# Attention's instructions on three engines tied to a written order, scores in two parts around the transposes, normalization a step later

## Chip, core and metric

One Trainium2 chip; the program runs on one of its cores. The metric is the device time of one execution in microseconds (us). A core has TensorE (PE in the profile, its weight loads PEld), VectorE (DVE), ScalarE (ACT), GpSimd (POOL) and SyncE (SP). Each engine takes its own instructions in the order in which they stand in its stream; an instruction that waits holds up all that stand behind it on that engine.

## What is computed

One layer of a streaming encoder on 1024 tokens of width 1024: a projection to queries, keys, values and an SSM input; differential attention over 4 heads of two score maps each; an S5 state-space mixer with a gated linear unit (GLU); an output projection with layer norm; a mixture of 32 experts with a second layer norm. The change touches attention, the end of the GLU and nothing else:

```python
# per block of 128 queries, head h, the two maps c = 0, 1 (chunk-block-causal mask)
sc = einsum('bqhcd,bkhcd->bhcqk', qi, k) * scale
p = softmax(where(mask, sc, -inf))
attn = p[:, :, 0] - lam * p[:, :, 1]
o = einsum('bhqk,bkhe->bqhe', attn, v)
o = o * rsqrt(mean(o**2) + RMS_EPS) * subln_g * (1 - lam_init)
# GLU behind the S5 mixer
z = gelu(y); z = z * sigmoid(z @ w_glu + b_glu)
```

## The kernel before

Attention is cut into 32 units (h, i): head h and the block i of 128 queries, which sees n = 128(i+1) keys. `units` lists heads 0 and 1 first, alternating a wide block of head 0 with a narrow one of head 1, (0,7), (1,0), (0,6), (1,1), ..., and then heads 2 and 3 together from block 7 down to block 0. In what follows unit u is the u-th of this list, counted from 0, and step u is one turn of the loop over them, which computes the scores of unit u+2 (`LEAD` is 2) and weighs the values of unit u.

- `scores` (L781 to L811): TensorE multiplies queries and keys into a tile `s` (L792 and L793, each product in two parts for precision). VectorE sets the masked corner (L801 or L809) and takes the negative maximum into `nm` (L802 or L810). ScalarE takes the exponential into `p` and its sum into `L` (L795). With n up to 512 both maps share one `s` tile; with more each map has one, and the three engines are gone through once for each map. The `s` tiles come from `bank2`, which has two buffers.
- `weigh` (L814 to L830): VectorE takes the reciprocal of `L`, a small factor `rho` and then p0 + rho p1 (all through the helper `stt`, L163). TensorE transposes the result (`at`, L826); ScalarE copies the first four blocks of it from PSUM and VectorE the others (L827); TensorE multiplies by the values into `po` (L830). Four blocks of a head share one `po`.
- `normalize` (L832 to L855): after a group of four blocks ScalarE copies `po` and squares it, VectorE sums and scales in small instructions on 128x4 numbers (`ss`), GpSimd takes the power -1/2 and multiplies. `finish` transposes (`ot`, L852) and ScalarE writes `aoT` (L853).
- `FILLS` puts other work behind given steps: `ask` (queries of heads 2 and 3, with casts on ScalarE, subtractions on GpSimd and DMAs), `glu_prepare` (loads w_glu into `wg_raw`, casts on ScalarE, subtractions on GpSimd), eight `glu` parts (12 products each on TensorE, a tanh on ScalarE, a scaling on GpSimd, and a multiplication of `zT` on VectorE) behind steps 16 to 19 and 21 to 24, and `wo_part` (four quarters of w_out through `wo_raw`).

The 128x2048 tiles of all these are slots of a first-in, first-out list (`Slots`), so a load waits until the tile that had its slot before has been read. What sets the order within attention is the compiler's scheduler, which merges all of this by its own estimates of time. Only behind the routing, in the experts, does the kernel write its order out: `keep_order` there makes each instruction follow the one traced before it on its engine. After attention come the output projection (`mix`, L1082) with the routing and then the experts.

Of the kernel before, what the change touches and what calls it, by code (L numbers as in the profile page):

```python
# [19 lines left out]
P = 128  # L20
# [93 lines left out]
def tile_kernel(ctx: ExitStack, tc: tile.TileContext, I: dict, out: bass.AP, dbg=None):  # L114
# [624 lines left out]
    def glu(ct, half):  # L739
# [12 lines left out]
        mul(z_, z_, sg)  # L752
# [10 lines left out]
    ts(gcol, gcol, 1.0 - LAM_INIT, ALU.mult)  # L763
    aoT = {}

    def sm(name, n, bufs=4):
        return cp.tile([P, n], F32, tag=name, name=name, bufs=bufs)

# [14 lines left out]
    def scores(h, i, qd, L, j):  # L783
# [13 lines left out]
        if n <= 512:  # L797
            s2 = bank2(f"s{h}_{i}").rearrange("p (c n) -> p c n", c=2)
            for c in range(2):
                products(s2[:, c, :], c)  # L800
            V.memset(s2[0:64, :, n - 64:n], -1e30)  # L801
            V.tensor_reduce(out=nm, in_=s2[:, :, 0:n], axis=AX.X, op=ALU.max, negate=True)  # L802
            for c in range(2):
                weights(s2[:, c, :], c)
        else:
            for c in range(2):
                s_ = bank2(f"s{h}_{i}_{c}")
                products(s_, c)
                V.memset(s_[0:64, n - 64:n], -1e30)  # L809
                V.tensor_reduce(out=nm[:, c:c + 1], in_=s_[:, 0:n], axis=AX.X, op=ALU.max, negate=True)  # L810
                weights(s_, c)  # L811
        return p_

    def weigh(h, i, p_, L, RL, j, po):  # L814
# [5 lines left out]
        stt(p_[:, 0, 0:n], p_[:, 1, 0:n], rho, p_[:, 0, 0:n], ALU.mult, ALU.add)  # L820
        aT = half.get("aT", [8, P], bufs=2)
# [6 lines left out]
        sl.put(p_)  # L828
        for k in range(i + 1):
            PE.matmul(po[:, j * P:(j + 1) * P], aT[:, k, :], vv[k // 4][:, k % 4, h * P:(h + 1) * P],  # L830
                      start=(k == 0), stop=(k == i))

    def normalize(h, g, po, RL):
# [5 lines left out]
        ss = sm("ss", 4, 2)  # L839
        V.tensor_reduce(out=ss, in_=sq[:, 0, :].rearrange("p (j e) -> p j e", j=4), axis=AX.X, op=ALU.add)  # L840
        r0 = RL[:, :, 0]
        mul(ss, ss, r0)
        mul(ss, ss, r0)
        ts(ss, ss, 1.0 / P, ALU.mult, EPS, ALU.add)
        G.tensor_tensor(out=ss, in0=ss, in1=mhalf, op=ALU.pow)
        mul(ss, ss, r0)
        mul(o4, o4, ss.unsqueeze(2).broadcast_to([P, 4, P]), G)
# [7 lines left out]
        return finish  # L855
# [16 lines left out]
    def start(u):  # L872
# [6 lines left out]
        live[u] = scores(h, i, qd[h], grp[h, i // 4][0], i % 4)  # L879
        starts[h] = starts.get(h, 0) + 1  # L880
        if starts[h] == NT:
            sl.put(*qd.pop(h), kk.pop(h))

# [19 lines left out]
    late = {}  # L903
    for u in range(LEAD):
        start(u)
    for u, (h, i) in enumerate(units):
        if u + LEAD < len(units):
            start(u + LEAD)
        L_, RL_, po_ = grp[h, i // 4]
        weigh(h, i, live.pop(u), L_, RL_, i % 4, po_)  # L910
# [3 lines left out]
        if ends[h, i // 4] == 4:  # L914
            late[u + LATE] = normalize(h, i // 4, po_, RL_)
        if u in fills:
            for f_, *a_ in fills[u]:
                {"ask": ask, "pre": glu_prepare, "glu": glu, "wo": wo_part}[f_](*a_)
    for f_ in late.values():
        f_()  # L920
    sl.put(*vv.values())
# [418 lines left out]
    def keep_order():  # L1340

        traced, prev = nc.cur_bb.bb.instructions, {}
        at = next(k for k, i in enumerate(traced) if i is pins[0])
        for i in traced[at:]:
            if i.engine not in ORDERED:
                continue
            if i.engine in prev:
                tc.add_manual_dep(i, prev[i.engine].name,
                                  mybir.DependencyInfo(mybir.DependencyClass.NoSync, mybir.DependencyReason.DATA),
                                  reason="keep_order")  # L1350
            prev[i.engine] = i
# [273 lines left out]
```

## Time and profile before

| what | us |
|---|---|
| median of 3 runs | 1177.47 (1177.21 to 1180.05) |
| profiled execution | 1178.13 |
| its span in the trace | 1176.4 |
| scores of unit 2 to scores of unit 31 (attention's body) | 282.93 to 416.24 |
| first product of the output projection | 417.94 |

Over the whole span TensorE is busy 92%, VectorE 82%, ScalarE 60%, GpSimd 30%. The shares are means over stages of different kind: the projection and the SSM come first, then attention from 273 to about 440 us, the projection out and the routing to about 560 us, and then the experts, in which TensorE is busy nearly throughout. Times within the trace are counted from the start of the span. A row of the timeline gives start, duration, engine, source line, operation, output and inputs, and in brackets how long the engine sat idle before it and what ended that.

### The profile page before, as it was taken

How to read it: one execution, taken by the hardware profiler on the slowest of the kernel's cores; microseconds unless marked ns; L12 is line 12 of the kernel's file. 1: busy time of each engine (PE TensorE's matmuls, PEld its weight loads, DVE VectorE, ACT ScalarE, POOL GpSimd, SP SyncE). 2: the span in 40 equal slices, each digit the busy share in tenths (PEclk: the TensorE clock that was granted, in tenths of full speed). 3: DMA queues.
4: the chain of work that ended last, by engine and by line, in shares of the span. 5: the costliest groups of instructions: out<-in, count | busy, mean ns of one | idle time of the engine just before them, and what ended most of it. 6: DMA issues, size and time to landing. Idle time of an engine off the chain costs nothing.

```text
span 1176.4 us, 15227 instructions
## 1 busy us (share of the span) xinstructions
PE 1083.7 (92%) x5345; PEld 903.9 (77%) x5345; DVE 970.0 (82%) x1434; ACT 708.5 (60%) x956; POOL 358.0 (30%) x296
## 2 busy tenths in 40 slices
PE   6979998897869989995999999999999999999994
PEld 5867887676758878885888888888888888888862
DVE  4898567556878785456899999999999999999976
ACT  3312332426756653212788888888888888888852
POOL 1077464312453454243121221221221211211133
PEclk9989999898999999996999999999999999999997
DMA  8537321201120346446599999999999999999593
GB/s 209 138 97 259 113 59 29 59 19 41 40 64 4 130 160 217 168 171 242 195 343 386 374 380 389 382 393 392 367 393 381 362 384 379 387 392 386 191 261 149
DMA packets 90686, 278.90 MB, mean 237 GB/s; under 512 B 29468, under 2 KB 49964, under 8 KB 66160
## 3 DMA queue, kind: packets, MB, share of 16 engines
q1 hardware_dynamic: 78080, 252.78, 57.6%
q0 software_dynamic: 11520, 24.83, 7.8%
q8 instruction: 43, 0.70, 0.2%
q10 hardware_dynamic: 1008, 0.30, 0.1%
q14 instruction: 35, 0.29, 0.1%
HBM read 254.12 MB, written 34.60 MB: 245 GB/s over the span
## 4 chain that ended last, share of the span: by engine, by line
PE 69%; DVE 12%; DMA 7%; ACT 4%; SPq 3%; issue 3%; POOL 1%; ACTq 0%; DVEq 0%; POOLq 0%
PE g L1251 15%; PE y L1242 15%; PE u L1251 14%; PE mix L1082 7%; PE proj L243 4%; DMA misc<-in_w_in_dram 3%; PE xT L1212 3%; DMA moe_dram<-zero 2%; PE glu L745 2%; PE po L830 2%; DVE ssm L157 1%; SPq L581 1%; PE hT L1224 1%; PE s L792 1%; PE pl L1104 1%
## 5 line engine op out<-in xcount | busy, mean ns | idle before, releaser
L1151 POOL DMA_INDIRECT moe_dram<-yo,idx x30 | 52.1, 1738 | 425.9 <-DVE yo L163 425.9
L243 PE MATMUL proj<-xh,wa 128*128 128x512 f32 x256 | 77.9, 412 | 4.4 <-ACT ssm L678 4.2
L243 PE MATMUL proj<-xh,wb 128*128 128x512 f32 x256 | 74.5, 404 | 1.6 <-ACT ssm L678 1.6
L1082 PE MATMUL mix<-woh,mx 128*128 128x512 f32 x256 | 73.8, 399 | 1.6 <-DVE mx L154 1.6
L1146 POOL DMA_INDIRECT gx<-h_dram,idx x32 | 60.4, 1889 | 22.5 <-DVE WT L160 13.1
L795 ACT ACTIVATE p<-s,nm 128x1024 f32<-128x1024 f32 (+7 forms) x64 | 47.2, 743 | 24.3 <-DVE nm L810 14.9
L243 PEld LDWEIGHTS proj<-xh,wa 128*128 128x128 f32 x256 | 50.2, 199 | 14.9 <-ACT ssm L678 4.5
L243 PEld LDWEIGHTS proj<-xh,wb 128*128 128x128 f32 x256 | 48.6, 194 | 11.5 <-ACT ssm L678 1.8
L1082 PEld LDWEIGHTS mix<-woh,mx 128*128 128x128 f32 x256 | 47.4, 189 | 11.2 <-DVE mx L154 2.1
L792 PE MATMUL s<-kk,qh 128*128 128x512 f32 (+3 forms) x96 | 37.6, 396 | 18.1 <-ACT p L795 15.0
L1258 ACT ACTIVATE yo<-y,WT 128x1024 f32<-128x1024 f32 (+1 forms) x33 | 36.0, 1091 | 24.4 <-PE y L1242 24.4
L1212 PEld LDWEIGHTS xT<-ident,gx 128*128 128x128 f32 x256 | 36.2, 208 | 9.7 <-DMA gx<-h_dram,idx 5.7
L243 PE MATMUL proj<-xl,wa 128*128 128x512 f32 x128 | 43.6, 412 | 0.0
L1212 PE MATMUL xT<-ident,gx 128*128 128x128 f32 x256 | 36.9, 287 | 6.9 <-DMA gx<-h_dram,idx 5.4
L163 DVE SCALAR_TENSOR_TENSOR yo<-gx,first,yo 128x1024 f32<-128x1024 f32 (+1 forms) x33 | 41.3, 1252 | 1.6
L154 DVE TENSOR_TENSOR xe<-xT,xe 128x1024 fp32r<-128x1024 f32 (+1 forms) x33 | 39.1, 1184 | 4.1 <-ACT xe L173 4.1
L830 PE MATMUL po<-vv,half 128*128 128x128 f32 x288 | 41.0, 285 | 1.4 <-ACT half L827 1.3
L1082 PE MATMUL mix<-wol,mx 128*128 128x512 f32 x128 | 42.1, 397 | 0.0
L243 PE MATMUL proj<-xl,wb 128*128 128x512 f32 x128 | 41.0, 397 | 0.0
L173 ACT CAST xe<-xT 128x1024 fp32r<-128x1024 f32 (+1 forms) x33 | 32.3, 978 | 13.4 <-PE xT L1212 13.4
L830 PEld LDWEIGHTS po<-vv,half 128*128 128x128 f32 x288 | 37.4, 198 | 3.5 <-ACT half L827 2.4
L792 PEld LDWEIGHTS s<-kk,qh 128*128 128x128 f32 x96 | 19.3, 201 | 24.7 <-ACT p L795 22.6
(864 smaller groups left out, 3560.1 us busy)
## 6 DMA issues: line engine op xcount, KB each, us to landing
misc<-in_w_in_dram SPq DMA_DIRECT2D x16, 512.0 KB, 3.9
moe_dram<-zero SPq DMA_DIRECT2D x8, 1024.0 KB, 8.5
xr<-in_x_dram SPq DMA_DIRECT2D x8, 512.0 KB, 8.8
wo_raw<-in_w_out_dram SPq DMA_DIRECT2D x4, 1024.0 KB, 5.1
xa<-in_x_dram SPq DMA_DIRECT2D x8, 512.0 KB, 4.4
h_dram<-xa SPq DMA_DIRECT2D x8, 512.0 KB, 3.6
mo<-moe_dram SPq DMA_DIRECT2D x8, 512.0 KB, 8.6
mo<-moe_dram POOLq DMA_DIRECT2D x8, 512.0 KB, 12.7
```

The lines of the kernel that those rows point to most:

```text
L154: eng.tensor_tensor(out=out_, in0=a, in1=b, op=ALU.subtract)
L163: return V.scalar_tensor_tensor(out=out_, in0=a, scalar=s, in1=b, op0=op0, op1=op1)
L243: PE.matmul(o[:, hs], wt[kt // 4][:, w_, kt % 4, :], x_[:, hs], start=(kt == 0 and n == 0), stop=(kt == KT - 1 and n == 2))
L792: PE.matmul(s_[:, c0:c0 + w], qd[0][:, c, tk], kk[h][:, c, c0:c0 + w], start=True, stop=False)
L795: S.activation(p_[:, c, 0:n], s_[:, 0:n], AF.Exp, bias=nm[:, c:c + 1], accum_out=L[:, j, c:c + 1])
L830: PE.matmul(po[:, j * P:(j + 1) * P], aT[:, k, :], vv[k // 4][:, k % 4, h * P:(h + 1) * P], start=(k == 0), stop=(k == i))
L1082: PE.matmul(o[-(hs.start > 0)][:, hs], mx[:, m_, kt, :], (woh, wol)[w_][kt // 2][:, kt % 2, hs], start=(kt == 0 and n == 0), stop=(kt == K ...
L1146: return G.indirect_dma_start(out=dst, out_offset=None, in_=h_dram[:, :], in_offset=bass.IndirectOffsetOnAxis(ap=ix, axis=0), bounds_check ...
L1151: G.indirect_dma_start(out=moe_dram[:, :], out_offset=bass.IndirectOffsetOnAxis(ap=ix, axis=0), in_=src, in_offset=None, bounds_check=2 * ...
L1212: PE.transpose(b_[:, kt * P:(kt + 1) * P], rows(g_, kt), ident)
L1242: PE.matmul(y[h_], hid[e][:, x_, kt, :], w_[:, k, HALVES[h_]], start=(kt == 0 and n == 0), stop=(kt == 3 and n == 2))
L1251: PE.matmul(o, xT[e][:, x_, kt, :], w_[:, k, :], start=(kt == 0 and n == 0), stop=(kt == KT - 1 and n == 2))
```

## The change

- A new function `tie` holds the loop that `keep_order` had, and is called for attention too: every instruction of TensorE, ScalarE and VectorE that is traced from the first unit's scores to the last `finish` must follow the one traced before it on its engine. Left out of it are the instructions of `ask`, `glu_prepare` and `wo_part`; those of `glu` are in it. GpSimd and SyncE aren't tied.
- `scores`, `start` and `weigh` become generators, and the loop interleaves them by hand: (1) VectorE's part of `weigh` for unit u; (2) scores of unit u+2, of the first map where n is over 512, of both maps otherwise, with maximum and exponential; (3) transposes of unit u and their copies; (4) `normalize` of a group that ended a step earlier; (5) the second map's scores; (6) the sums and the scaling of that normalization; (7) the products with the values of unit u; then `finish`, then fills.
- `normalize` is given `L` in place of its reciprocal: it adds 128 eps L0^2 to the sum of squares (two small instructions for it and one addition), in place of three multiplications and a two-operation scaling, with sqrt(128) moved into `gcol`.
- The GLU's last multiplication goes from VectorE to GpSimd.

```diff
@@ glu
-        mul(z_, z_, sg)
+        mul(z_, z_, sg, G)
@@
-    ts(gcol, gcol, 1.0 - LAM_INIT, ALU.mult)
+    ts(gcol, gcol, (1.0 - LAM_INIT) * math.sqrt(P), ALU.mult)
+    def tie(traced, engines):
+        prev = {}
+        for i in traced:
+            if i.engine not in engines:
+                continue
+            if i.engine in prev:
+                tc.add_manual_dep(i, prev[i.engine].name,
+                                  mybir.DependencyInfo(mybir.DependencyClass.NoSync, mybir.DependencyReason.DATA),
+                                  reason="keep_order")
+            prev[i.engine] = i
@@ scores
             for c in range(2):
                 weights(s2[:, c, :], c)
-        else:
-            for c in range(2):
...
+            yield p_
+        for c in range(2 if n > 512 else 0):
+            s_ = bank2(f"s{h}_{i}_{c}")
+            products(s_, c)
...
+            weights(s_, c)
+            yield p_
@@ weigh
         stt(p_[:, 0, 0:n], p_[:, 1, 0:n], rho, p_[:, 0, 0:n], ALU.mult, ALU.add)
+        yield
...
         sl.put(p_)
+        yield
         for k in range(i + 1):
             PE.matmul(po[:, j * P:(j + 1) * P], aT[:, k, :], vv[k // 4][:, k % 4, h * P:(h + 1) * P],
@@ normalize
-        ss = sm("ss", 4, 2)
-        V.tensor_reduce(out=ss, in_=sq[:, 0, :].rearrange("p (j e) -> p j e", j=4), axis=AX.X, op=ALU.add)
-        r0 = RL[:, :, 0]
-        mul(ss, ss, r0)
-        mul(ss, ss, r0)
-        ts(ss, ss, 1.0 / P, ALU.mult, EPS, ALU.add)
-        G.tensor_tensor(out=ss, in0=ss, in1=mhalf, op=ALU.pow)
-        mul(ss, ss, r0)
-        mul(o4, o4, ss.unsqueeze(2).broadcast_to([P, 4, P]), G)
+        ss, l2 = sm("ss", 4, 2), sm("l2", 4, 2)
+        mul(l2, L[:, :, 0], L[:, :, 0])
+        ts(l2, l2, EPS * P, ALU.mult)
+        def scale():
+            V.tensor_reduce(out=ss, in_=sq[:, 0, :].rearrange("p (j e) -> p j e", j=4), axis=AX.X, op=ALU.add)
+            add(ss, ss, l2)
+            G.tensor_tensor(out=ss, in0=ss, in1=mhalf, op=ALU.pow)
+            mul(o4, o4, ss.unsqueeze(2).broadcast_to([P, 4, P]), G)
@@ the loop
-        if u + LEAD < len(units):
-            start(u + LEAD)
-        weigh(h, i, live.pop(u), L_, RL_, i % 4, po_)
+        old = weigh(h, i, live.pop(u), L_, RL_, i % 4, po_)
+        new = start(u + LEAD) if u + LEAD < len(units) else iter(())
+        next(old)
+        next(new, None)
+        next(old)
+        scales = [normalize(*done.pop(x)) for x in list(done)]
+        next(new, None)
+        for sc, fin in scales:
+            sc()
+            late[u + LATE - 1] = fin
+        next(old)
...
+                if f_ != "glu":
+                    apart.update(range(at, len(nc.cur_bb.bb.instructions)))
...
+    tie([i for k, i in enumerate(nc.cur_bb.bb.instructions) if k >= first_pin and k not in apart],
+        (mybir.EngineType.PE, mybir.EngineType.Activation, mybir.EngineType.DVE))
```

Three places show what this does to the streams. The first is TensorE at step 20, unit (2,5), while the scores of unit 23, (3,4), are next. In the names s_4_0 and s_4_1 are the first and second map's scores of a block 4, at_5 the transposes of a block 5, po_7_2596 (po_7_2600 after the change) the product with the values of head 2, and kk_2065 the keys of head 3. Before:

```order
L826 MATMUL at_5_0_2964<-ident,p_5_2824 128x128 x4
L792 MATMUL s_4_0_2988<-kk_2065,qh_2544 128x512
L793 MATMUL s_4_0_2988<-kk_2065,ql_2545 128x512
L792 MATMUL s_4_0_2988<-kk_2065,qh_2544 128x128
L793 MATMUL s_4_0_2988<-kk_2065,ql_2545 128x128
L826 MATMUL at_5_4_2970<-ident,p_5_2824 128x128 x2
L792 MATMUL s_4_1_2996<-kk_2065,qh_2544 128x512
L793 MATMUL s_4_1_2996<-kk_2065,ql_2545 128x512
L792 MATMUL s_4_1_2996<-kk_2065,qh_2544 128x128
L793 MATMUL s_4_1_2996<-kk_2065,ql_2545 128x128
L826 MATMUL at_5_0_3008<-ident,p_5_2886 128x128 x4
L830 MATMUL po_7_2596<-vv_1403,half_2070 128x128 x4
```

The product with the values of unit 20 stands behind both parts of unit 23's scores and behind transposes of unit 21. After:

```order
L839 MATMUL at_5_0_2956<-ident,p_5_2828 128x128 x4
L839 MATMUL at_5_4_2962<-ident,p_5_2828 128x128 x2
L804 MATMUL s_4_1_2966<-kk_2006,qh_2324 128x512
L805 MATMUL s_4_1_2966<-kk_2006,ql_2325 128x512
L804 MATMUL s_4_1_2966<-kk_2006,qh_2324 128x128
L805 MATMUL s_4_1_2966<-kk_2006,ql_2325 128x128
L844 MATMUL po_7_2600<-vv_1403,half_2070 128x128 x4
L844 MATMUL po_7_2600<-vv_1404,half_2070 128x128 x2
L804 MATMUL s_4_0_2992<-kk_2065,qh_2544 128x512
L805 MATMUL s_4_0_2992<-kk_2065,ql_2545 128x512
L804 MATMUL s_4_0_2992<-kk_2065,qh_2544 128x128
L805 MATMUL s_4_0_2992<-kk_2065,ql_2545 128x128
```

It now stands directly behind the second part of unit 22's scores, and unit 23's scores stand behind it. The second place is ScalarE at the same steps. Before:

```order
L795 ACTIVATE p_4_2942,L<-s_4_0_2944,nm 128x640
L749 ACTIVATE wg_raw<-glu_0_2926,bg 128x512
L795 ACTIVATE p_4_2942,L<-s_4_1_2952,nm 128x640
L827 COPY half_2070<-at_5_0_2964 128x512
L173 CAST woh_3100<-wo_raw_3098 128x1024
L795 ACTIVATE p_4_2986,L<-s_4_0_2988,nm 128x640
L827 COPY half_2070<-at_5_0_3008 128x512
```

Both exponentials of unit 22 come ahead of the copy of unit 20's transposes. After:

```order
L749 ACTIVATE wg_raw<-glu_0_2926,bg 128x512
L807 ACTIVATE p_4_2946,L<-s_4_0_2948,nm 128x640
L840 COPY half_2070<-at_5_0_2956 128x512
L807 ACTIVATE p_4_2946,L<-s_4_1_2966,nm 128x640
L173 CAST woh_3090<-wo_raw_3088 128x1024 x2
L807 ACTIVATE p_4_2990,L<-s_4_0_2992,nm 128x640
```

The copy has moved between the two exponentials of unit 22. The third place is ScalarE around steps 12 and 13, where the casts of w_glu (`wgh`) and of the SSM's output (`zh`) stand, and s_7_0 is the first part of unit 15's scores. Before:

```order
L795 ACTIVATE p_0_2523,L<-s_0_2525,nm 128x128 x2
L173 CAST zh_2696<-zT_763 128x1024
L173 CAST zh_2696<-zT_1282 128x1024
L827 COPY half_2070<-at_6_0_2576 128x512
L173 CAST wgh<-wg_raw 128x1024 x2
L795 ACTIVATE p_7_2554,L<-s_7_0_2556,nm 128x1024
```

After:

```order
L807 ACTIVATE p_0_2527,L<-s_0_2529,nm 128x128 x2
L840 COPY half_2070<-at_1_0_2538 128x256
L173 CAST wgh<-wg_raw 128x1024 x2
L173 CAST zh_2686<-zT_763 128x1024
L173 CAST zh_2686<-zT_1282 128x1024
L807 ACTIVATE p_7_2558,L<-s_7_0_2560,nm 128x1024
```

All four casts now stand ahead of unit 15's first exponential, and the copy of at_6 has gone behind it.

## Rows read from the trace of the kernel before

**Rows 1.** Stretches: length, busy us of PE, PEld, DVE, ACT, POOL, clock, DMA share, GB/s.
```profile
282.93:416.24 133.31, 111.51 (x691) 96.60 (x691) 110.51 (x228) 85.82 (x182) 53.99 (x41) 0.97 0.21 64
352.00:416.24 64.24, 59.28 (x367) 51.74 (x367) 52.35 (x108) 40.74 (x84) 25.48 (x20) 1.00 0.25 82
```
**Rows 2.** Timeline of TensorE: first products of units 2, 18 and 31.
```profile
282.93 0.79 PE L792 MATMUL s<-kk,qh 128*128 128x512 f32 x1 [2.13 <-ACT p L795]
...
352.00 0.50 PE L792 MATMUL s<-kk,qh 128*128 128x512 f32 x1
...
416.24 0.33 PE L792 MATMUL s<-kk,qh 128*128 128x128 f32 x1 [3.06 <-DVE p L163]
```
**Rows 3.** Chain that ended last: start, us; a value product, a GLU part, a score.
```profile
355.36 2.75 PE glu L745 x12
358.10 0.23 PE s L792
...
358.90 0.89 PE po L830 x8
```
**Rows 4.** Timeline of all engines: hand-overs from engine to engine.
```profile
302.75 0.40 PE L793 MATMUL s<-kk,ql 128*128 128x512 f32 x1
...
303.51 1.23 DVE L802 TENSOR_REDUCE nm<-s 128x2 f32<-128x1024 f32 x1
...
304.83 0.69 ACT L795 ACTIVATE p<-s,nm 128x512 f32<-128x512 f32 x1
...
309.50 0.59 ACT L827 COPY half<-at 128x512 f32<-128x512 f32 x1
...
310.14 1.16 PE L830 MATMUL po<-vv,half 128*128 128x128 f32 x8
```
**Rows 5.** Groups by line, 270 to 445 us: count, busy us, mean ns, idle before.
```profile
L795 ACT ACTIVATE p<-s,nm 128x1024 f32<-128x1024 f32 (+7 forms) x64 | 47.2, 743 | 24.3 <-DVE nm L810 14.9 <-DVE nm L802 7.0 <-DVE RL L817 2.1
...
L810 DVE TENSOR_REDUCE nm<-s 128x1 f32<-128x1024 f32 (+3 forms) x32 | 32.5, 1017 | 0.4
...
L827 ACT COPY half<-at 128x512 f32<-128x512 f32 (+3 forms) x32 | 16.2, 506 | 21.8 <-PE at L826 21.8
...
L802 DVE TENSOR_REDUCE nm<-s 128x2 f32<-128x256 f32 (+3 forms) x16 | 13.1, 818 | 0.3
...
L173 ACT CAST woh<-wo_raw 128x1024 fp32r<-128x1024 f32 x8 | 8.1, 1053 | 3.3 <-DMA wo_raw<-in_w_out_dram 2.7 <-DVE zT L157 0.6
...
L157 DVE TENSOR_TENSOR ss<-ss,RL 128x4 f32<-128x4 f32 x23 | 7.4, 325 | 2.3 <-POOL ss L845 2.1
L157 POOL TENSOR_TENSOR half<-half,ss 128x512 f32<-128x512 f32 x7 | 7.3, 1043 | 7.1 <-DVE RL L817 4.0 <-DVE ss L157 3.1
L157 DVE TENSOR_TENSOR zT<-zT,wg_raw 128x512 f32<-128x512 f32 x8 | 7.0, 872 | 0.6 <-POOL wg_raw L169 0.5
```
**Rows 6.** Groups by line and shape: widest and narrowest exponential with n over 512.
```profile
L795 ACT ACTIVATE p<-s,nm 128x1024 f32<-128x1024 f32 x8 | 8.9, 1113 | 4.4 <-DVE nm L810 4.4
...
L795 ACT ACTIVATE p<-s,nm 128x640 f32<-128x640 f32 x8 | 6.4, 796 | 5.2 <-DVE nm L810 4.2 <-DVE RL L817 0.9
```
**Rows 7.** SyncE's queue, waits: total us, times, longest.
```profile
SPq L729 <- PE s L793: 100.6, 1, 100.6
```
**Rows 8.** Chain that ended last, at the load of w_glu.
```profile
332.19 5.62 DMA wg_raw<-in_w_glu_dram
```
**Rows 9.** Timeline of all engines, VectorE beside GpSimd's subtraction.
```profile
321.31 2.62 DVE L163 SCALAR_TENSOR_TENSOR rho<-L,nlam,RL 128x1 f32<-128x1 f32 x1
321.53 4.79 POOL L154 TENSOR_TENSOR ql<-qr,qh 64x1024 fp32r<-64x1024 f32 x2
...
323.97 3.17 DVE L163 SCALAR_TENSOR_TENSOR p<-p,rho 128x768 f32<-128x768 f32 x1
```
**Rows 10.** Stretch of 10 us with the gap before unit 31.
```profile
410.00:420.00 10.00, 6.75 (x39) 5.67 (x39) 9.71 (x25) 6.43 (x21) 5.81 (x5) 0.84 0.58 199
```
**Rows 11.** Timeline of TensorE: a shorter gap.
```profile
345.00 0.51 PE L792 MATMUL s<-kk,qh 128*128 128x512 f32 x1 [1.55 <-ACT p L795]
```

More of the change, by code (lines that the diff above doesn't have):

```diff
@@ L804, in scores @@
                 weights(s2[:, c, :], c)
-        else:
-            for c in range(2):
[L807 to L812, printed above, removed]
+            yield p_
+        for c in range(2 if n > 512 else 0):
+            s_ = bank2(f"s{h}_{i}_{c}")
+            products(s_, c)
+            V.memset(s_[0:64, n - 64:n], -1e30)
+            V.tensor_reduce(out=nm[:, c:c + 1], in_=s_[:, 0:n], axis=AX.X, op=ALU.max, negate=True)
+            weights(s_, c)
+            yield p_
     def weigh(h, i, p_, L, RL, j, po):
@@ L831, in weigh, with normalize @@
                       start=(k == 0), stop=(k == i))
-    def normalize(h, g, po, RL):
+        yield
+    def normalize(h, g, po, L):
         sq = half.get("sq", [2, 512], bufs=2)
@@ L853, in finish @@
             S.mul(aoT[g][:, h, :], b_, gcol)
-        return finish
+        return scale, finish
     proj_k(0)
@@ L878, in start @@
                               sm("RL", 8, 4).rearrange("p (j c) -> p j c", c=2), bank(f"po{h}_{i}", 1))
-        live[u] = scores(h, i, qd[h], grp[h, i // 4][0], i % 4)
+        live[u] = steps = scores(h, i, qd[h], grp[h, i // 4][0], i % 4)
+        p_ = next(steps)
+        yield
+        for _ in steps:
+            pass
+        live[u] = p_
         starts[h] = starts.get(h, 0) + 1
@@ L882, in start @@
             sl.put(*qd.pop(h), kk.pop(h))
+        yield
     woh, wol = [], []
@@ L903, in tile_kernel @@
     late = {}
+    first_pin = len(nc.cur_bb.bb.instructions)
     for u in range(LEAD):
-        start(u)
+        for _ in start(u):
+            pass
+    done, apart = {}, set()
     for u, (h, i) in enumerate(units):
-        if u + LEAD < len(units):
-            start(u + LEAD)
         L_, RL_, po_ = grp[h, i // 4]
-        weigh(h, i, live.pop(u), L_, RL_, i % 4, po_)
+        old = weigh(h, i, live.pop(u), L_, RL_, i % 4, po_)
[9 more added lines that the diff above has]
+        next(old)
         if u in late:
@@ L914, in tile_kernel @@
         if ends[h, i // 4] == 4:
-            late[u + LATE] = normalize(h, i // 4, po_, RL_)
+            done[u] = h, i // 4, po_, L_
         if u in fills:
             for f_, *a_ in fills[u]:
+                at = len(nc.cur_bb.bb.instructions)
                 {"ask": ask, "pre": glu_prepare, "glu": glu, "wo": wo_part}[f_](*a_)
+                if f_ != "glu":
+                    apart.update(range(at, len(nc.cur_bb.bb.instructions)))
+    for x in list(done):
+        sc, fin = normalize(*done.pop(x))
+        sc()
+        late[len(units) + x] = fin
     for f_ in late.values():
         f_()
+    tie([i for k, i in enumerate(nc.cur_bb.bb.instructions) if k >= first_pin and k not in apart],
+        (mybir.EngineType.PE, mybir.EngineType.Activation, mybir.EngineType.DVE))
     sl.put(*vv.values())
@@ L1340, in keep_order @@
     def keep_order():
[L1342 to L1351, printed above, removed]
+        traced = nc.cur_bb.bb.instructions
+        tie(traced[next(k for k, i in enumerate(traced) if i is pins[0]):], ORDERED)
     def refill():
```

## Prediction

> **What bounds the kernel now.** I first read the table of stretches over attention's body, from the scores of unit 2 to those of unit 31 [rows 1, 2]. It lasts 133.31 us, in which TensorE is busy 111.51 us and VectorE 110.51 us. So two engines are nearly full, and neither has to wait long for the other. In the second part, from 352.00 us on, TensorE has work for 59.28 of 64.24 us. That works only because the stream of TensorE runs ahead. The first order listing above shows how: unit 20's product with the values stands behind both parts of unit 23's scores, so TensorE computes scores while ScalarE still prepares that product. Attention isn't a stage whose loss is made up later: projection out, routing and experts follow it, and I expect its change in length to appear in full at the end.
>
> **The order that the change writes, as a chain.** After the change each step u has these dependencies, read from the new order listings. TensorE does the scores of unit u+2 (first map, or both where n is up to 512). VectorE takes their maximum. ScalarE takes their exponential. Only behind that exponential on ScalarE stands the copy of unit u's transposes. TensorE's product of unit u with the values needs that copy, and behind the product on TensorE stand the GLU part, if any, and then the first scores of unit u+3. So no step can be shorter than this chain, whatever else the engines have to do; in the waits TensorE has only the transposes of unit u and the second part of the scores. From the scores of unit 2 to those of unit 31 there are 29 such steps, 0 to 28. I add up the chain's members over them, at durations of the profile:
>
> - First-part scores: a product of 512 columns takes 0.23 us [rows 3], narrower ones by width (an estimate from that row). 15 wide units give 3 x 0.92 + 4 x 0.80 + 4 x 0.69 + 4 x 0.57 = 11.0, 14 narrow ones 4 x 0.92 + 4 x 0.69 + 4 x 0.46 + 2 x 0.23 = 8.7. Together 19.7 us.
> - From the last product's issue to the maximum: its result ends 0.40 after its start, 0.17 later than the next could have started, and the maximum starts 0.36 later still, the masking included (303.51 less 303.15) [rows 4]. 29 x 0.5 (a little under the 0.53, as the mask of one map is smaller) = 14.5 us.
> - Maxima: half of the 32 single ones, less the one of unit 0 at 1.2, is 15.0; of the 16 double ones the 14 that fall in are 12.2 [rows 5]. 27.2 us.
> - Exponentials: the four wide shapes average about 0.955, half-way between 1.113 and 0.796 [rows 6]; 16 of them less one of 1.113 are 14.2. The narrow ones are 47.2 less 32 x 0.955 = 16.6 [rows 5], less four of the narrowest (about 0.35 each) 15.2. 29.4 us.
> - Hand-overs to ScalarE and back to TensorE, 0.09 and 0.05 [rows 4]: 4.1 us.
> - Copies: 16.2 for 32 [rows 5], less three narrow ones: 15.3 us.
> - Products with the values: 8 records take 0.89 [rows 3]; 280 of the 288 records fall in: 31.1 us.
> - Eight GLU parts of 2.75 [rows 3] and six groups of four transposes at 0.11, as long as a value record: 24.7 us.
>
> The sum is 166.0 us against 133.3 before: **plus 32.7 us**. Checked against one step: step 16 (weigh a block 7, score a block 6, one GLU part) gives 0.80 + 0.5 + 1.09 + 0.14 + 1.01 + 0.59 + 1.79 + 2.75 = 8.7, of which TensorE has work for 7.1.
>
> **What else the change does.** *Loads that ScalarE waits for.* In the third order listing the casts of w_glu and the SSM's output, four of 1.05 us, stand ahead of unit 15's first exponential. The load takes a slot that unit 14's scores free; SyncE waits for them in the profile already [rows 7], and it lands 5.62 us after issue [rows 8]. From the start of unit 14's scores: 0.45 + 0.24 + 5.6 + 4.2 = 10.5 us until that exponential, which the chain would reach after 2.9 + 0.9 + 0.5 + 1.2 + 0.1 = 5.6: plus 4.9. Similarly the last quarter of w_out takes the slot of unit (3,2)'s `p`, is issued after that unit's transposes, and its two casts stand ahead of unit 30's exponential: 0.8 + 0.2 + 5.6 + 2.1 = 8.7 against 5.2, plus 3.5. The other cast pairs (queries twice, the second half of the SSM's output, three quarters of w_out), about 2.1 us each [rows 5], fall where ScalarE is free for 1 to 2 us of the chain: 0.3 to 1.3 each, 4 together. **Plus 12.4**, between 8 (the two computed stalls alone) and 17.
>
> *VectorE.* Taken off: 8 multiplications of the GLU at 0.87, 7.0 us, and the four small ones per group become two off the path to `ss` and one on it; 23 of the old cost 7.4 us with 2.1 of waiting for GpSimd [rows 5]. I count the gain as nothing: with the written order VectorE has about 110 us of work in 166, and the chain covers it. If it were not covered, the gain would be at most 7.0 + 4 + 2 = 13 us.
>
> *GpSimd beside VectorE.* The profile shows what a subtraction on GpSimd does to VectorE: `rho`, 0.2 us otherwise, took 2.62, and the sum over two `p` took 3.17 [rows 9], together some 4.7 too long. In the written order VectorE can't go on with a maximum meanwhile, and the maximum is in the chain; about 1.7 us of slack stand before it. At three places (queries of heads 2 and 3, GLU preparation) that is 0 to 3 us each; I take 1.7, half-way: **plus 5**, bounds 0 and 9. The Trainium skill, SBUF — State Buffer, section "Who interferes with whom", speaks here against the change: VectorE with two inputs in SBUF and GpSimd share a port pair that is locked for a whole instruction. The rows of `rho` and `p` agree. By that rule the 8 GLU multiplications, now on GpSimd at 1.04 each (the row of the like-sized multiplication there [rows 5]), could hold VectorE for 8.3 us, and the sum would be 1241; I leave them at nothing, as GLU steps have the most slack.
>
> *TensorE's clock.* The gap of 3.06 us before unit 31 [rows 2] lies in a stretch with a granted clock of 0.84 [rows 10], a mean of 2.4 and 1.2 GHz; the first products of unit 2, at 0.79 for 512 columns, are at the lower level too, while the gap of 1.55 us left those behind it at 0.51 [rows 11]. In the chain most steps have gaps of 1.5 to 2.4 us, but those that score a block with n = 384 or 512 have 2.9 to 3.4 (0.5 + 1.2 + 1.4 + 0.6 less the transposes), eight of them, and the load above some 6. Their nearest row is that of 3.06. A step at the lower level costs 1.6 us more in the first half and 4.7 more with a GLU part. If all eight fall, about 25; if none, nothing. As transposes and second parts split many gaps, I take two falls: **plus 6**, bounds 0 and 25.
>
> Sum against the profiled execution of 1178.13: 1178.1 + 32.7 + 12.4 + 5 + 6 = 1234.2; its distance to the median, 0.66, taken off: **1233.5 us**, 4.8% slower.
>
> **Rivals.**
> *VectorE's relief decides (faster).* If ScalarE and TensorE were always ahead in the written order, a step would last as long as VectorE's work, and each of the 13 us taken off would count, less those where TensorE was full anyway (352 to 408 us). Some 9 us would be left: 1168. For it: VectorE busy 110.51 of 133.31 [rows 1]. Against: the copy behind the exponential. It decides only where the chain of a step is below VectorE's work in it, about 5.0 us at a block 7 and 2 at a narrow one; the chain has 6.2 and 4.
> *The scheduler's order was nearly this one.* ScalarE's stream before has many copies between two exponentials too. If the chain bound only a third of the steps, plus 11 and half of the load stalls: about 1195. Against: the listings, in which the product before scores is the rule after the change. Were even that order unchanged, 1177.
> *The clock stays low.* If idle time keeps TensorE at 1.2 GHz for half of the stretch, half of its 75 us in the chain doubles, plus 38 in place of 6: 1266. For it: idle time of about a third. Against: the short gaps around 345 us at full clock.
>
> **How the numbers follow.** About 0.3% is what a measurement of this kernel can tell from no change. Chances: forecast, within 1203 to 1258, 0.70; order nearly as before, 1182 to 1203, 0.10; low clock, above 1258, 0.10; no change within 0.3%, 0.03; VectorE's relief, 0.07. The range takes in the forecast's bounds and reaches into both slower rivals: 1192 to 1264, leaving out about 0.18. Slower by over 0.3% is 0.70 + 0.10 + 0.10 = 0.90, within it 0.03, faster 0.07.
>
> **What would show it.** In the profile of the changed kernel: units 2 to 31 take some 180 to 190 us; TensorE's longest waits are value products for the copy (line 840), ScalarE's are for maxima; the copy starts at the end of the exponential of unit u+2; VectorE's busy share in the stretch falls to about 60%; the last part of the kernel keeps its length. I am wrong if value products don't wait for that copy, or if the stretch is shorter than 166 us, which the chain doesn't allow.

## The result, and the profile after

The changed kernel takes 1245.86 us (median; 1243.86 to 1246.63) against 1178.42 for the kernel before, measured beside it: a ratio of 1.058, 95% interval 1.0558 to 1.0601, or 67.4 us more. The prediction was 1233.5 us with a range of 1192 to 1264. Direction and mechanism were right; 12 us were missing.

The profiled execution took 1246.63 us, its span is 1244.9. Stretches of the changed kernel: length, busy us of PE, PEld, DVE, ACT, POOL, granted clock, DMA share, GB/s. The first goes from unit 2's scores to unit 31's, the second from there to the end.

```profile
282.30:482.92 200.62, 136.10 (x716) 115.99 (x717) 112.08 (x220) 93.07 (x193) 74.26 (x56) 0.83 0.16 48
482.92:1244.90 761.98, 727.05 (x3425) 604.04 (x3424) 659.02 (x793) 522.19 (x614) 176.19 (x138) 0.97 0.83 314
```

Attention's body grew from the 133.31 us of [rows 1] to 200.62, by 67.3 of the 68.5 us that the span grew. All that follows it is 1.8 us longer (760.16 us before, counted in the same way). VectorE is busy about as long as before, 112.08 us against 110.51, and now for 56% of the stretch. The GLU multiplications are gone from it (seven of them took 5.6 us in that stretch before), but the sums over two `p` (L163) take 36.7 us in place of 26.8, as more of them now run beside an instruction of GpSimd and last longer for it (rows below); `rho`, in turn, takes 10.4 in place of 15.5. TensorE's busy time went up by 24.6 us with almost the same products (716 records in place of 691, as 16 value products and 9 transposes more fall into the stretch), and its granted clock fell from 0.97 to 0.83. What TensorE waited for in that stretch (total us, times, longest):

```profile
PE po L844 <- ACT half L840: 60.1, 27, 5.6
PE at L839 <- DVE p L163: 3.4, 4, 1.5
PE s L804 <- ACT p L807: 2.5, 1, 2.5
PE at L839 <- DVE s L821: 1.0, 1, 1.0
```

Of 67.0 us, 60.1 are products with the values that wait for ScalarE's copy (line 840). Step 20, from all engines' timeline (start, us; in brackets the idle time ahead and its releaser), shows how the chain goes round:

```profile
415.86 0.39 PE L804 MATMUL s<-kk,qh 128*128 128x512 f32 x1
...
416.37 0.28 PE L805 MATMUL s<-kk,ql 128*128 128x128 f32 x1
...
416.94 0.82 DVE L822 TENSOR_REDUCE nm<-s 128x1 f32<-128x640 f32 x1
...
417.86 0.79 ACT L807 ACTIVATE p<-s,nm 128x640 f32<-128x640 f32 x1 [1.12 <-DVE nm L822]
...
418.65 0.58 ACT L840 COPY half<-at 128x512 f32<-128x512 f32 x1
...
419.27 1.60 PE L844 MATMUL po<-vv,half 128*128 128x128 f32 x12 [1.31 <-ACT half L840]
...
420.64 0.48 PE L804 MATMUL s<-kk,qh 128*128 128x512 f32 x1
```

Unit 22's first scores, their maximum, their exponential, then the copy of unit 20's transposes, then unit 20's product, then unit 23's scores: each starts within 0.3 us of the end of the one before. The transposes that the copy reads were issued at 416.48 and are 0.84 us long, so they were there more than a microsecond before 418.65. The step lasted 4.78 us. By the members that the prediction adds up (scores, hand-over, maximum, hand-overs, exponential, copy, product) it is 0.57 + 0.50 + 0.82 + 0.14 + 0.79 + 0.59 + 1.33 = 4.74.

The clock is the next thing to see: the same kind of work behind a wait of 1.41 us and behind one of 3.11, from TensorE's timeline, and under it two stretches of 10 us.

```profile
411.42 1.83 PE L844 MATMUL po<-vv,half 128*128 128x128 f32 x14 [1.41 <-ACT half L840]
413.01 0.47 PE L745 MATMUL glu<-zh,wgh 128*128 128x512 f32 x1
413.32 0.39 PE L745 MATMUL glu<-zl,wgh 128*128 128x512 f32 x1
...
433.09 1.90 PE L844 MATMUL po<-vv,half 128*128 128x128 f32 x10 [3.11 <-ACT half L840]
434.64 0.77 PE L745 MATMUL glu<-zh,wgh 128*128 128x512 f32 x1
435.21 0.63 PE L745 MATMUL glu<-zl,wgh 128*128 128x512 f32 x1
```
```profile
402.00:412.00 10.00, 7.73 (x50) 6.88 (x51) 6.46 (x12) 5.18 (x11) 7.52 (x5) 1.00 0.00 0
442.00:452.00 10.00, 6.85 (x30) 5.82 (x30) 3.99 (x9) 4.87 (x10) 3.94 (x4) 0.83 0.54 206
```

After the longer wait 10 product records take longer than 14 do after the shorter one, and the second GLU product 0.63 instead of 0.39: TensorE is at its lower level (1.2 of 2.4 GHz) there; the clock granted from 434.6 to 435.8 is 0.50. I measured the price over the whole stretch in TensorE's timeline: 29 pieces, each from the start of a value product to the end of the scores that open the next step. The end is the start of the last score product plus 0.23 us for 512 columns at full clock, twice that at the lower level (287.20 to 289.57 is the first piece). Together they last 95.4 us. At full clock, by the prediction's members, they are 31.1 + 24.7 + 19.1 = 74.9, where 19.1 is its 19.7 for the first-part scores with unit 31's in place of unit 2's. Of the 20.5 us between them, 14 pieces carry nearly all (0.6 to 2.0 us each, 18.5 together), and they stand behind waits of 1.88 to 5.58 us or directly behind another such piece. The length of the wait alone doesn't decide. Behind 2.75 us (394.05) and behind 3.22 (316.24) a piece lost nothing, while the one behind 1.88 (475.62) lost 1.2 us, with the clock at 0.50 since the piece before it. In the profile of e10 below, the product that answers to 394.05 waited 2.74 us too, and its piece lost 1.7.

The loads that ScalarE waits for are there as well. Timeline around w_glu's casts and around those of the last quarter of w_out:

```profile
359.36 1.99 ACT L173 CAST wgh<-wg_raw 128x1024 fp32r<-128x1024 f32 x2 [3.46 <-DMA wg_raw<-in_w_glu_dram]
...
361.26 1.99 ACT L173 CAST zh<-zT 128x1024 fp32r<-128x1024 f32 x2
...
363.15 1.11 ACT L807 ACTIVATE p<-s,nm 128x1024 f32<-128x1024 f32 x1
...
364.87 3.36 PE L844 MATMUL po<-vv,half 128*128 128x128 f32 x14 [5.58 <-ACT half L840]
```
```profile
479.03 1.99 ACT L173 CAST woh<-wo_raw 128x1024 fp32r<-128x1024 f32 x2 [3.46 <-DMA wo_raw<-in_w_out_dram]
```

Unit 15's first maximum was done at 359.04; its exponential began 4.1 us later, behind four casts of which the first waited for its load. The step lasted 11.46 us (356.42 to 367.88). The casts of w_out above stand ahead of unit 30's exponential in the same way: its maximum was done at 478.74, and it began at 480.93.

### The profile page after: what moved, and what is told of

Its sections match the earlier page's. It is cut to its first block, busy times and chain, and to the rows that moved or that the text cites. A ratio compares the mean times of both kernels' runs of the same rounds, so it can differ in the third digit from the quotient of the medians.

```text
span 1244.9 us, 15256 instructions
## 1 busy us (share of the span) xinstructions
PE 1105.4 (89%) x5345; PEld 921.0 (74%) x5345; DVE 963.6 (77%) x1418; ACT 708.7 (57%) x956; POOL 369.0 (30%) x304
## 4 chain that ended last, share of the span: by engine, by line
PE 67%; DVE 12%; DMA 7%; ACT 6%; issue 4%; SPq 3%; POOL 1%; ACTq 0%; DVEq 0%; POOLq 0%
PE g L1293 14%; PE y L1284 14%; PE u L1293 14%; PE mix L1124 7%; PE proj L243 4%; PE po L844 3%; DMA misc<-in_w_in_dram 3%; PE xT L1254 3%; PE glu L745 2%; DMA moe_dram<-zero 2%; ACT p L807 2%; DVE ssm L157 1%; SPq L581 1%; PE hT L1266 1%; PE pl L1146 1%
## 5 line engine op out<-in xcount | busy, mean ns | idle before, releaser
L844 PE MATMUL po<-vv,half 128*128 128x128 f32 x288 | 48.9, 325 | 60.1 <-ACT half L840 60.1
L844 PEld LDWEIGHTS po<-vv,half 128*128 128x128 f32 x288 | 42.2, 226 | 68.2 <-ACT half L840 68.0
L804 PE MATMUL s<-kk,qh 128*128 128x512 f32 (+3 forms) x96 | 40.9, 428 | 5.8 <-ACT p L807 5.8
L163 DVE SCALAR_TENSOR_TENSOR yo<-gx,first,yo 128x1024 f32<-128x1024 f32 (+1 forms) x33 | 41.3, 1252 | 1.6
L163 DVE SCALAR_TENSOR_TENSOR p<-p,rho 128x1024 f32<-128x1024 f32 (+7 forms) x32 | 37.4, 1170 | 1.4 <-DVE rho L163 0.3
## 6 DMA issues: line engine op xcount, KB each, us to landing
mo<-moe_dram SPq DMA_DIRECT2D x8, 512.0 KB, 10.8
```

What stands on the lines that cost most here:

```text
L163: return V.scalar_tensor_tensor(out=out_, in0=a, scalar=s, in1=b, op0=op0, op1=op1)
L804: PE.matmul(s_[:, c0:c0 + w], qd[0][:, c, tk], kk[h][:, c, c0:c0 + w], start=True, stop=False)
```

## The experiments

My theory had three parts: a chain through ScalarE's copy, loads ahead of exponentials, and a lower clock that follows TensorE's idle time. The rivals: the moved pieces themselves cost, not their order; the loads and the clock carry most of it, the chain a third; any fixed order loses. Each kernel ran in 3 or 5 rounds beside the kernel before. Ratios are to the kernel before, with 95% intervals.

| kernel | us | ratio |
|---|---|---|
| changed | 1245.86 | 1.0580 (1.0558 to 1.0601) |
| e1, no order in attention | 1182.44 | 1.0057 (1.0035 to 1.0079) |
| e2, copy ahead of the exponential | 1200.33 | 1.0196 (1.0174 to 1.0219) |
| e3, value products a step later | 1195.62 | 1.0155 (1.0133 to 1.0176) |
| e4, TensorE free | 1200.08 | 1.0200 (1.0182 to 1.0218) |
| e5, idle work in TensorE's waits | 1236.99 | 1.0505 (1.0475 to 1.0535) |
| e6, casts at their place | 1233.40 | 1.0469 (1.0445 to 1.0494) |
| e7, VectorE free | 1247.62 | 1.0591 (1.0565 to 1.0617) |
| e8, before, GLU multiplication on GpSimd | 1180.12 | 1.0020 (1.0004 to 1.0035) |
| e9, e3 + e6 + e7 | 1189.34 | 1.0099 (1.0065 to 1.0134) |
| e10, subtractions of queries and GLU on VectorE | 1247.92 | 1.0598 (1.0565 to 1.0631) |
| e11, e1 with that multiplication on VectorE | 1182.89 | 1.0043 (1.0022 to 1.0063) |
| e12, before, new normalization formula | 1183.75 | 1.0044 (1.0023 to 1.0066) |

**e1: the written order taken away.**

```diff
-    tie([i for k, i in enumerate(nc.cur_bb.bb.instructions) if k >= first_pin and k not in apart],
-        (mybir.EngineType.PE, mybir.EngineType.Activation, mybir.EngineType.DVE))
```

> The changed kernel without the written order in attention: the call of tie over attention is left out, all else of the change (scores in two parts around the transposes, normalization a step later, GLU multiplications on GpSimd) stays. Theory (the written order makes a chain through ScalarE's copy behind the next exponential, and idle time and clock follow from it): 1170 to 1185 us, and TensorE's waits for the copy fall from 60 us to under 10. Rival (the moved pieces cost, not the order): above 1215 us.

1182.44 us: 63.4 of the 67.4 us are gone with this one call. The stretch from unit 2 to unit 31 in e1, and two of TensorE's waits (275 to 460 us):

```profile
282.37:417.36 134.99, 115.32 (x691) 99.70 (x691) 109.37 (x215) 85.97 (x182) 65.63 (x51) 0.94 0.21 61
```
```profile
PE s L804 <- ACT p L807: 14.7, 14, 3.3
...
PE po L844 <- ACT half L840: 0.5, 2, 0.2
```

Of the waits of value products for the copy 0.5 us are left. So the order costs, and not the pieces, but for some 5 us (below).

**e2: the link cut on ScalarE.**

```diff
+        f0 = len(nc.cur_bb.bb.instructions)
         next(new, None)
+        f1 = len(nc.cur_bb.bb.instructions)
         next(old)
+        moved.append((f0, f1, len(nc.cur_bb.bb.instructions)))
...
+    for f0, f1, f2 in moved:
+        act = [k for k in range(f0, f2) if seq[k].engine == mybir.EngineType.Activation]
+        for k, new_k in zip(act, [k for k in act if k >= f1] + [k for k in act if k < f1]):
+            where[k] = new_k
```

> The changed kernel with one link of the chain cut: in ScalarE's written order the copy of unit u's transposes stands ahead of the first exponential of unit u+2 instead of behind it; the orders of TensorE and VectorE stay as they are. Theory (the chain through that copy sets the step, and the clock falls because TensorE waits for it): 1180 to 1205 us, since the stalls on loads (some 12 us) stay. Rival (the stalls on loads, the clock and VectorE beside GpSimd carry most of the loss, the chain only a third): 1225 to 1245 us. Second rival (any fixed order loses, since engines can't step around each other): above 1215 us.

1200.33 us: swapping one copy with one or two exponentials in each step of ScalarE's list gives back 45.5 us, with all three engines still in a fixed order. TensorE's waits in e2:

```profile
PE at L839 <- DVE p L163: 16.1, 10, 5.4
PE po L844 <- ACT half L840: 11.1, 15, 1.7
```

The wait for the copy fell from 60.1 to 11.1 us. Both rivals, as the expectation puts them, fall; but e2 is still 2.0% slower than the kernel before, so that a smaller cost of any fixed order isn't excluded.

**e3: the link cut on TensorE.**

```diff
-        next(old)
+        held.append((old, h, i, po_, L_))
+        if len(held) > 1:
+            value(u, *held.pop(0))
```

> The changed kernel with the chain cut on TensorE: the product of unit u with the values, and the normalization behind it, come one step later in the written order, so that the scores of unit u+3 stand ahead of it; ScalarE keeps the copy behind the exponential. Theory: the copy then has a whole step of cover, 1180 to 1205 us, and the clock granted in the stretch comes back above 0.92. Rival (ScalarE's order itself, with the load casts in it, is the bound): 1225 to 1245 us.

1195.62 us, 50.2 less than the changed kernel. The clock of the stretch came back to 0.90, a little under the 0.92 expected. A second link of the same kind is now the longest (timeline of e3):

```profile
321.11 0.63 ACT L853 ACTIVATE half<-half 128x512 f32<-128x512 f32 x1
...
321.77 0.69 DVE L860 TENSOR_REDUCE ss<-half 128x4 f32<-128x512 f32 x1 [2.71 <-ACT half L853]
...
323.02 0.89 DVE L163 SCALAR_TENSOR_TENSOR p<-p,rho 128x640 f32<-128x640 f32 x1
...
323.96 1.33 PE L839 MATMUL at<-ident,p 128*128 128x128 f32 x5 [4.06 <-DVE p L163]
```

The sum of squares waits on VectorE for ScalarE's square; `p`, which doesn't need it, stands behind it in the written order, and TensorE's transposes wait 4.06 us for `p`.

**e4 and e7: which engines' order it takes.**

```diff
-        (mybir.EngineType.PE, mybir.EngineType.Activation, mybir.EngineType.DVE))
+        (mybir.EngineType.Activation, mybir.EngineType.DVE))
```

> The changed kernel with the written order kept on ScalarE and VectorE alone: TensorE's is left to the scheduler, which again puts most products with the values behind the scores of unit u+3. Theory (the chain needs TensorE's place for the product as well): 1180 to 1205 us. Rival (ScalarE's and VectorE's orders alone already bind): 1225 to 1245 us.

> The changed kernel with the written order kept on TensorE and ScalarE, VectorE left to the scheduler. Theory (the chain needs the orders of TensorE and ScalarE alone): 1235 to 1250 us. Rival (VectorE's maximum held up in its own fixed order carries part of the loss): below 1225 us.

e4 (the diff) took 1200.08 us, e7 (`DVE` left out instead of `PE`) 1247.62. With TensorE free the scheduler puts the product of unit u behind the first scores of unit u+3 in all 29 steps (in 19 of them in the kernel before, in none in the changed kernel, counted in the traces), and the chain is gone although ScalarE keeps its order. With VectorE free nothing is won, and the wait for the copy is as long (e7, 280 to 480 us):

```profile
PE po L844 <- ACT half L840: 64.7, 25, 4.8
```

The chain needs the orders of TensorE and ScalarE, and not VectorE's. ScalarE alone was not freed; what its order does is seen in e2.

**e5: the clock.**

```diff
+            if k1 == i + 1 and k1 - k0 < 4 and narrow:
+                for _ in range(12):
+                    PE.transpose(b_[:, 3 * P:4 * P], ident, ident)
             (V.tensor_copy if k0 else S.copy)(aT[:, k0:k1, :], b_[:, 0:(k1 - k0) * P].rearrange("p (k q) -> p k q", q=P))
```

> The changed kernel with idle work put into TensorE's waits: in steps where the scores of unit u+2 are narrow (one part), and the last group of unit u's transposes leaves columns of its bank free, 12 transposes of the identity into those free columns follow them, 11 steps, at 0.11 us each at full clock and some 0.21 at the lower level. Their result is read by nobody. Theory on the clock (the loss of some 20 us in TensorE's blocks behind its waits comes from the lower granted clock that follows idle time): the granted clock of the stretch rises above the 0.83 of the changed kernel, the products behind these waits get shorter, and the time falls by 4 to 12 us. Rival (the lower clock has another cause than idle time, or the products behind a wait are slow for another reason): no change or up to 10 us longer.

`narrow` says that unit u+2's scores come in one part; eleven steps get the 12 transposes (132 records more in the stretch). 1236.99 us: 8.9 us faster by doing more work. Step 22's product and first GLU products in e5, which answer to 433.09 and 434.64 above, and the whole stretch:

```profile
428.95 1.38 PE L847 MATMUL po<-vv,half 128*128 128x128 f32 x10 [1.80 <-ACT half L843]
430.09 0.48 PE L745 MATMUL glu<-zh,wgh 128*128 128x512 f32 x1
430.40 0.40 PE L745 MATMUL glu<-zl,wgh 128*128 128x512 f32 x1
```
```profile
281.75:473.55 191.80, 136.95 (x848) 118.70 (x849) 112.25 (x220) 93.10 (x193) 73.98 (x56) 0.93 0.18 51
```

The clock rose from 0.83 to 0.93, and the excess of the 29 pieces over full clock fell from 20.5 to 9.3 us. The stretch is 8.8 us shorter, as the rest of it grew by some 2 us. So filling the idle time did raise the clock here, and the lower clock does stand on the path.

**e6: the loads.**

```diff
-ASK, GLU, WO = (6, 12), (15, 16, 1, 20, 21, 1), (22, 24, 26, 30)
+ASK, GLU, WO = (6, 12), (13, 16, 1, 20, 21, 1), (22, 24, 26, 30)
...
-                if f_ != "glu":
-                    apart.update(range(at, len(nc.cur_bb.bb.instructions)))
```

> The changed kernel with the casts of loaded data tied in as well, at the place where they are written (behind the exponentials of their step), and the preparation of the first GLU half two steps earlier: no cast whose load is still under way stands ahead of an exponential any more. Theory (loads that ScalarE waits for cost 8 to 17 us, most of it at the casts of w_glu and the last quarter of w_out): 4 to 10 us faster than the changed kernel, since the casts' own time of about 2 us a pair stays on ScalarE; ScalarE's wait for the load of w_glu is gone. Rival (the chain would have waited there anyway, for the clock or for VectorE beside GpSimd): within 3 us of the changed kernel.

1233.40 us, 12.5 less than the changed kernel, more than the 4 to 10 expected. ScalarE in e6:

```profile
355.02 1.11 ACT L807 ACTIVATE p<-s,nm 128x1024 f32<-128x1024 f32 x1 [0.94 <-DVE RL L829]
...
356.13 1.98 ACT L173 CAST wgh<-wg_raw 128x1024 fp32r<-128x1024 f32 x2
358.02 1.98 ACT L173 CAST zh<-zT 128x1024 fp32r<-128x1024 f32 x2
```

The casts now stand behind unit 15's exponentials and wait for nothing. Not all of the 12.5 us are the stalls' own: the excess of the pieces fell from 20.5 to 14.5 us too. In e6's trace the stretch is 189.56 us, 11.1 shorter: 6 of them in TensorE's pieces, at a clock less often low, and 5 in the rest.

**e10: subtractions on VectorE.**

```diff
-            sub(lo[a, c, :], src[a], hi[a, c, :].bitcast(F32), G)
+            sub(lo[a, c, :], src[a], hi[a, c, :].bitcast(F32), V if h > 1 else G)
...
-                split(wgh[:, js, :], wgl[:, js, :], raw[:, js, :], G)
+                split(wgh[:, js, :], wgl[:, js, :], raw[:, js, :], V)
```

(and in the same way for `zh`). The eight subtractions of w_out, which the expectation names as well, were not moved: in e10's trace they are still on GpSimd, 18.9 us of work.

> The changed kernel with the subtractions that split queries of heads 2 and 3, the GLU's operands and w_out on VectorE instead of GpSimd. Theory (a subtraction on GpSimd holds up a VectorE instruction that runs beside it, and in the written order that delay stands in the chain): 2 to 8 us faster, since VectorE has time left over. Rival (such delays fall where ScalarE waits for the casts anyway): within 2 us of the changed kernel, or slower by up to 5 us, since VectorE then does about 16 us more itself.

1247.92 us, not to be told from the changed kernel. As VectorE does more itself in e10, this bounds only the sum of the two effects, and only for the queries and the GLU's operands; the trace of the changed kernel says the rest (below).

**e8, e11, e12: what is left without the order.** e8 is the kernel before with `mul(z_, z_, sg, G)`; e11 is e1 with that line back on VectorE; e12 is the kernel before with the new formula of `normalize` at its old place:

```diff
+        mul(l2, L[:, :, 0], L[:, :, 0])
+        ts(l2, l2, EPS * P, ALU.mult)
...
-        mul(ss, ss, r0)
-        mul(ss, ss, r0)
-        ts(ss, ss, 1.0 / P, ALU.mult, EPS, ALU.add)
+        add(ss, ss, l2)
         G.tensor_tensor(out=ss, in0=ss, in1=mhalf, op=ALU.pow)
-        mul(ss, ss, r0)
```

> The kernel before with one line of the change alone: the 8 multiplications of the GLU's gate with its input go from VectorE to GpSimd. Without the written order the change lost 5 us (experiment e1). Theory A (this line costs it, GpSimd holding VectorE up or the gate's result later): 3 to 6 us slower than before. Theory B (the order in which the scheduler sees the pieces, or the normalization, costs it): within 2 us of before, or up to 4 us faster, since VectorE has 7 us less to do.

> As e1 (no written order in attention), with the 8 GLU multiplications back on VectorE; left of the change are the scores in two parts and the normalization a step later. Against e1's 1182.4 and before's 1177.3 it splits the 5 us: if the GLU's line carries half of it, as e8 points to (plus 2.4), 1179 to 1181; if all lies in the pieces and their order, 1182 to 1184.

> The kernel before with the new formula of the normalization alone, at its old place in the program: the factor of L squared in the sum in place of three multiplications by the reciprocal. What is left of the 5 us that the change loses without a written order (e1, e11) lies either here or in the scores taken in two parts and the order in which the scheduler then sees the pieces. If the formula is free: 1174 to 1180 us (within 2 us of before, VectorE having at most 4 us less to do). If the formula costs it: 1180 to 1184 us.

The GLU line costs 0.5 to 4.1 us alone, between e8's two theories; taken out of e1, it gives nothing back (e11, 1182.89 against 1182.44), which is the second of e11's two cases. The formula alone costs 2.7 to 7.8 us (e12, "the formula costs it"), as much as e11 with everything but the order and the GLU line. So the pieces are worth a loss of about 5 us together, the single losses don't add up, and none brings a gain. Why a formula with less work for VectorE loses 0.4% under the scheduler stays open: the scheduler also reorders what stands around it, and no run here separates the two.

**e9: the losses taken out together.**

> The changed kernel with the three losses taken out together: the product of unit u with the values a step later (as in e3), the casts of loaded data tied at their place with the GLU preparation two steps earlier (as in e6), and VectorE left to the scheduler, since in e3 TensorE's longest waits were transposes waiting for VectorE's p, which stood in VectorE's written order behind a sum of squares that waited for ScalarE. Theory: the written order of TensorE and ScalarE is then no longer a chain; the stretch from unit 2 to unit 31 takes 130 to 145 us and the kernel 1172 to 1190 us. Rival (a fixed order on these two engines keeps costing some 10 us or more, as each wait on one holds up everything behind it): 1190 to 1205 us.

e9 is e3 with e6's edit, and VectorE free as in e7. 1189.34 us lies at the edge of both expectations, and its stretch of 149 us is longer than the 130 to 145 that the theory gave: inconclusive. Its waits are spread over many causes, the longest 9.5 us in all for scores that wait for exponentials, and its clock in the stretch is 0.88. No version here beats the kernel before.

## Why the prediction was right, and where it was short

**The chain (plus 32.7): right.** By its members the 29 steps take 166.0 us. Where neither clock nor load interferes, steps come out to within 0.1 us: 4.78 against 4.74 in step 20 above, 8.56 (399.14 to 407.70) against 8.5 in step 18. e2 and e4 cut it at its two places and got back 45 us each, chain and clock together.

**TensorE's clock (plus 6, bounds 0 and 25): the step that failed.** It measured 17 to 21 us: 20.5 in the 29 pieces, of which about 0.11 each, 3.2 together, is lost at full clock too, as in the pieces from 377 to 425 us. I had the mechanism and a bound that holds it, but took "two falls", because transposes and second parts split the gaps. Second parts exist only at wide units; at narrow ones TensorE has transposes of 0.3 to 1.3 us and then waits 1.8 to 3.7 us. In the first half about every second piece lost by the clock, and from step 22 on every one. The gap of 3.06 us [rows 2, 10] was the right row; I should have counted how many steps of the chain come near it instead of only those with n = 384 or 512. The rival of the low clock had put half of the stretch there, 38 us; the truth lies about half-way.

**Loads (plus 12.4): nearly right.** The four casts ahead of unit 15 made step 13 last 11.46 us; the chain alone makes it 6.0. Outside TensorE's own products, which the clock made 1.5 us longer, the casts cost 3.9 us where I had put 4.9. The last quarter of w_out cost 2.2 where I had put 3.5. Four other pairs of casts ahead of an exponential (steps 1, 17, 24 and 26) cost 0.9 to 1.3 us each, 4.7 together, where I had put 4. That is 10.8 in all. e6 won 12.5 us by mending these places, about half of it by way of the clock.

**GpSimd beside VectorE (plus 5, bounds 0 and 9): too much.** The changed kernel's timeline at the queries of heads 2 and 3:

```profile
296.63 4.80 POOL L154 TENSOR_TENSOR ql<-qr,qh 64x1024 fp32r<-64x1024 f32 x2 [3.72 <-PE at L839]
...
299.24 2.48 DVE L163 SCALAR_TENSOR_TENSOR p<-p,rho 128x256 f32<-128x256 f32 x1
...
301.94 0.96 DVE L814 TENSOR_REDUCE nm<-s 128x2 f32<-128x768 f32 x1
```
```profile
343.06 4.78 POOL L154 TENSOR_TENSOR ql<-qr,qh 64x1024 fp32r<-64x1024 f32 x2
...
345.48 3.18 DVE L163 SCALAR_TENSOR_TENSOR p<-p,rho 128x768 f32<-128x768 f32 x1
```

VectorE is held up as in [rows 9], but the delay meets the chain only at the first place: there the maximum starts at 301.94 though its scores were done at 300.38, some 1.2 us late. At the second, `p` ends at 348.66, before unit 13's first scores do. At w_glu it falls into the load's stall. That is about 1 us in place of 5. Not in the prediction at all is another delay in VectorE's order: in steps 8 and 16 the maximum stands behind the sum of squares of the normalization, which waits for ScalarE's square. This cost 1.1 and 0.7 us. The Trainium skill, SBUF — State Buffer, section "Who interferes with whom", tells why VectorE is held: an instruction of it with two inputs in SBUF and one of GpSimd that reads SBUF exclude each other on a shared port pair. These rows and those of [rows 9] agree. The 8.3 us that the prediction worked out from that rule for the GLU's multiplications (a sum of 1241.8, where it says 1241) did not come: in the chain, steps 18 to 23 are, outside TensorE's own products, within 0.1 us of their members. In the kernel before, where the scheduler sets the order, e8 measures 0.5 to 4.1 us for them.

**The GLU's multiplications on GpSimd (nothing): nearly.** One of them met the path in a way I had not seen: ScalarE's cast of the third quarter of w_out (`woh`) waits, by the profile, for GpSimd's last multiplication, the last reader of `wg_raw`, which stood behind a subtraction of 4.66 us. That `woh` has the slot of `wg_raw` would explain it, but no run here shows the slots:

```profile
459.48 4.66 POOL L154 TENSOR_TENSOR wol<-wo_raw,woh 128x1024 fp32r<-128x1024 f32 x2 [0.95 <-PE glu L745]
...
465.11 1.27 POOL L157 TENSOR_TENSOR zT<-zT,wg_raw 128x512 f32<-128x512 f32 x1
...
466.11 0.69 DVE L814 TENSOR_REDUCE nm<-s 128x2 f32<-128x512 f32 x1
466.41 1.99 ACT L173 CAST woh<-wo_raw 128x1024 fp32r<-128x1024 f32 x2 [0.73 <-POOL zT L157]
...
468.31 0.47 ACT L807 ACTIVATE p<-s,nm 128x256 f32<-128x256 f32 x1
```

The maximum was done at 466.80, the exponential came at 468.31: 1.5 us, of which the wait for GpSimd is 0.7 and the rest the casts' own time (it is step 26 above).

**The sum.** In the stretch I had forecast 133.3 + 32.7 + 12.4 + 5 + 6 = 189.4 us, and 200.6 were measured, 11.2 more. With unit 2's scores in place of unit 31's, as the stretch has them, TensorE's pieces are 96.3 us against 75.5 by the members, 20.8 more, which is 14.8 over the forecast of 6. The rest of the chain took 200.6 − 96.3 = 104.3 us against 90.5 by its members, 13.8 more, where loads and GpSimd had 17.4, 3.6 too many. 14.8 − 3.6 = 11.2. So the forecast came as near as it did partly by luck: too much for the loads and GpSimd made up for a quarter of what the clock lacked.

**The rivals.** VectorE's relief decided nothing: with VectorE free (e7) the time stays, and VectorE's busy share in the changed kernel is 56%. The order was not nearly the old one: 60.1 us of waits at one place. Of the forecast signs, the waits for the copy, the copy's start behind the exponential (418.65, as 417.86 + 0.79), ScalarE's waits for maxima (23.4 us for `nm` of L822, second only to the GLU's tanh), VectorE's share and the unchanged last part came out; the stretch was to be 180 to 190 us and is 200.6.

## What to carry to other kernels

When several engines are put into one written order, follow one step round: if an instruction that the next step's first work needs stands, on any engine, behind work that this step's first work has just released, the step is the sum of a chain and not the maximum of the engines' work. One swap on one of the two engines involved gave back 45 of 67 us here, so look for the link before giving up the order. And when a chain makes TensorE wait, count the waits one by one at the level of clock that follows them: that was 17 to 21 of the 67 us here.

## What the runs showed that I had not expected

TensorE won 8.9 us by work that nobody reads (e5): 12 transposes in each of eleven waits. Its clock followed not the length of the last wait alone: behind 2.75 us nothing was lost in the changed kernel and 1.7 us behind 2.74 at the same place in e10. Over the stretch TensorE was busy 0.68 of the time in the changed kernel at a granted clock of 0.83, and 0.71 in e5 at 0.93.
